# Both MLPs' last down-projection block as seven quarter products, under a written plan for all engines

## The chip, the core and the metric

The kernel runs on one core of a Trainium2 chip. A core has a matrix engine (TensorE, PE in the profile; its weight loads are PEld), a vector engine (VectorE, DVE), a scalar engine (ScalarE, ACT), a general one (GpSimd, POOL) and a sync engine (SyncE, SP) that mostly issues transfers. They run side by side, each through its own queue in order, and wait for one another by semaphores. Data lies in DRAM, in the on-chip SBUF (128 partitions) and in PSUM, eight banks of 128 partitions x 512 fp32 into which PE writes and adds. Sixteen DMA engines move data between DRAM and SBUF; a transfer can also add to what stands at its target (those are issued from POOL).

The metric is the device time of one execution in microseconds (us). It is compared as the median of several runs.

## The reference

Two decoder layers over 512 tokens of width 1024, all in fp32. Layer 0 mixes by latent attention, layer 1 by sliding-window attention; both go on with the same kind of MLP (width 4096) and a LayerNorm after each sublayer:

```python
def _mlp(x, w_up, w_down):
    h = jax.nn.relu(x @ w_up)
    return (h * h) @ w_down

for l in range(DEPTH):
    y = _mla(...) if l < n_a else _swa(...)
    x = _layernorm(alpha * x + y, ln_mix_g[l], ln_mix_b[l])
    x = _layernorm(alpha * x + _mlp(x, mlp_w_up[l], mlp_w_down[l]), ln_mlp_g[l], ln_mlp_b[l])
```

## The kernel before

Each fp32 operand of a product is split into a high part, rounded to the matmul's format (a copy on ACT, L77), and a low part, the difference (a subtraction, L81, on DVE or for some weights on POOL). A product takes three matmuls, high x high, high x low and low x high (`three`), all issued at L105 by `group`.

The MLP walks over its 4096 hidden features in four blocks q of 1024 (`NFF` = 4). In a block, "U" is the up projection and "D" the down projection. Both are made after Strassen's scheme in Winograd's form: tokens and features are cut in halves, the four quarters of each operand are combined by sums, and seven quarter products take the place of eight. They are numbered 1 to 7; `STEPS` is the order in which the steps run, with U' for the next block:

```python
STEPS = "U'1 D5 U'2 D3 U'5 D6 D7 U'3 D4 U'6 U'7 U'4 D'1 D'2"
FIRST_STEPS, LAST_STEPS = "U'1 U'2 U'5 U'3 U'6 U'7 U'4 D'1 D'2", "U'1 D5 U'2 D3 U'5 D6 D7 U'3 U'6 U'7 U'4 D4"
```

`Block.up` (L813) makes a U product of 48 matmuls of 256 columns in two halves and `up_out` (L836) its sums on DVE (L854 to L864), the ReLU and the square on ACT (L867, L868): the four quarters a11, a12, a21, a22 of the hidden activations. `Block.factor` (L871) makes a D product's left factor, a quarter or a sum of quarters (`Factors.sum`, L697: one sum for 5, two for 3, one for 7), split in two. `Block.down_` (L882) makes a D product, 24 matmuls of 512 columns for two token tiles, and adds its result to the tokens `xs` or to `u2` on DVE (L641, L792, L900). The sums of the weights' quarters are made by transfers: a quarter is loaded (SP), split, and the next quarter is added to it in SBUF by a DMA from POOL (L204, `add_more`).

The last block (q = 3) has D products of another kind: the plain product, all four token tiles against all eight weight chunks, made by `TokMajor.finish` (L547). It first makes the left 512 columns of all four tiles, then the right 512 tile by tile, so that the norm of one tile (`layer_norm`, L484: mean and variance by `bn_stats`, L631, and `bn_aggr`, L488; the reciprocal root on POOL, L443; two passes on DVE, L494 and L495) lies beside the product of the next. In layer 1 the last tile's right half is made in two pieces, and `last_norm` (L469) subtracts the mean for the first 512 columns by two matmuls (`ident`, `diag`), scales in three pieces on DVE (L481) and sends each out. In layer 0 the normed tiles are turned by PE (L507, `turn_tokens`) for the next layer, whose first products (w_k, w_v; `begin`, L657) lie between the turns of the last two tiles.

What sets the order: PE and the transfers of SP keep the order in which they are written (`pe`). DVE, ACT and POOL are ordered by a planner that runs when the program is built, by priorities and its own estimates of times; `pin` and `behind` fix single places. Weights come from a list (`stream`) that `weights` prepares at most four chunks ahead; `wh` and `wl` have four buffers each, factors (`fac`) three, PSUM six banks plus two for turns, and the eight large tiles `xt` hold the tokens' parts.

## Time and profile before

| | us |
|---|---|
| median of three runs | 987.31 (987.04 to 987.75) |
| the profiled execution | 986.77 |
| its span, first to last instruction | 985.0 |
| layer 0's MLP in the span, to its last block's U'6 | 206.7 to 436.8 |
| layer 1's MLP in the span, to its last block's U'6 | 681.3 to 911.4 |

The busy table gives each engine's time and share of the span. Matmuls are pipelined, so a PE that is "busy" isn't always at its peak; the chain of work that ended last, followed back from the last instruction, says better what sets the time. A line of that chain in order of time reads: start, length, engine, what it made and its source line, how many instructions. A line of an engine's timeline reads the same way, with operands (out <- in), shapes and, in brackets, the idle time before it and who ended it. A line of the groups has busy time, mean ns of one, idle time before and its releaser. The last figures of a windows row are granted clock, DMA share and GB/s.

### The profile page before, as it was taken

The numbers are of one execution on the slowest core, as the hardware profiler recorded it, in microseconds if no ns is written. First come the engines' busy times: TensorE is split into PE (matmuls) and PEld (weight loads), VectorE is DVE, ScalarE is ACT, GpSimd is POOL, SyncE is SP. The second block draws the span as 40 slices with busy tenths as digits, with TensorE's granted clock in tenths as the row PEclk, the third lists the DMA queues.
The fourth block names the chain that finished last, engine by engine and source line by source line (L and its number), as shares of the span: only waits on it lengthen the run. The fifth ranks groups of instructions, "written<-read, shape, count | busy, mean of one in ns | idle before, by whom it ended". The sixth has DMA issues, their size and how long they took to land.

```text
span 985.0 us, 15665 instructions
## 1 busy us (share of the span) xinstructions
PE 978.4 (99%) x6028; PEld 880.5 (89%) x6028; DVE 773.4 (79%) x1282; ACT 544.7 (55%) x842; POOL 235.7 (24%) x204
## 2 busy tenths in 40 slices
PE   9999999999999999999999999999999999999998
PEld 9888888998999999998898988889998998999986
DVE  6589858999778769887587788898886985888756
ACT  5557644467537637646136787445763763764720
POOL 1231101121212211310002898422221122033000
PEclk9999999999999999999999999999999999999999
DMA  7421236398878968973232212528997796897332
GB/s 264 146 89 44 91 124 199 59 225 218 156 181 235 183 141 237 226 125 120 94 108 86 97 65 98 191 44 181 256 179 134 236 197 117 225 264 140 82 128 86
DMA packets 60678, 149.54 MB, mean 152 GB/s; under 512 B 5259, under 2 KB 10300, under 8 KB 60604
## 3 DMA queue, kind: packets, MB, share of 16 engines
q0 software_dynamic: 24320, 58.73, 33.7%
q1 hardware_dynamic: 36140, 89.56, 26.0%
q8 instruction: 47, 0.77, 0.3%
q10 hardware_dynamic: 144, 0.26, 0.1%
q14 instruction: 27, 0.22, 0.1%
HBM read 146.41 MB, written 4.22 MB: 153 GB/s over the span
## 4 chain that ended last, share of the span: by engine, by line
PE 97%; DVE 2%; POOL 1%; ACT 0%; issue 0%; DVEq 0%; POOLq 0%
PE mm L105 89%; PE tr L105 5%; PE tr L1243 1%; PE tr L742 1%; POOL wl L81 1%; PE tr L1467 0%; PE tr L507 0%; DVE o L1503 0%; DVE mm L1431 0%; DVE pt L81 0%; PE tr L1007 0%; ACT wh L77 0%; DVE mm L1427 0%; PE mm L1148 0%; ACT p L1442 0%
## 5 line engine op out<-in xcount | busy, mean ns | idle before, releaser
L105 PE MATMUL mm<-wh,fac 128*128 128x512 f32 (+1 forms) x944 | 292.7, 386 | 0.0
L77 ACT ACTIVATE wh<-wq 128x1024 fp32r<-128x1024 f32 x164 | 173.7, 1060 | 184.7 <-PE mm L105 137.8
L81 DVE TENSOR_TENSOR wl<-wq,wh 128x1024 fp32r<-128x1024 f32 x164 | 199.2, 1220 | 67.5 <-ACT wh L77 66.6
L105 PE MATMUL mm<-xth,wh 128*128 128x256 f32 (+1 forms) x928 | 243.4, 290 | 0.0
L105 PE MATMUL mm<-xth,wl 128*128 128x256 f32 (+1 forms) x800 | 233.3, 292 | 0.0
L105 PEld LDWEIGHTS mm<-wh,fac 128*128 128x128 f32 x944 | 176.2, 188 | 35.5 <-DVE fac L81 0.6
L105 PE MATMUL mm<-xtl,wh 128*128 128x256 f32 (+1 forms) x672 | 197.1, 293 | 0.0
L105 PE MATMUL mm<-wl,fac 128*128 128x512 f32 (+1 forms) x472 | 182.3, 386 | 0.0
L105 PEld LDWEIGHTS mm<-xth,wh 128*128 128x128 f32 x928 | 168.6, 192 | 3.1
L105 PEld LDWEIGHTS mm<-xth,wl 128*128 128x128 f32 x800 | 153.2, 192 | 2.7
L105 PEld LDWEIGHTS mm<-xtl,wh 128*128 128x128 f32 x672 | 128.7, 191 | 3.0
L77 ACT ACTIVATE wh<-raw 128x1024 fp32r<-128x1024 f32 (+3 forms) x86 | 84.9, 989 | 79.3 <-PE mm L105 57.9
L204 POOL DMA_DIRECT2D wq<-in_up x64 | 77.6, 1238 | 200.3 <-DVE wl L81 193.0
L105 PEld LDWEIGHTS mm<-wl,fac 128*128 128x128 f32 x472 | 88.8, 188 | 16.6
L81 DVE TENSOR_TENSOR wl<-raw,wh 128x1024 fp32r<-128x1024 f32 (+2 forms) x64 | 74.3, 1169 | 30.6 <-ACT wh L77 29.6
L204 POOL DMA_DIRECT2D wq<-in_down x48 | 42.0, 874 | 189.1 <-DVE wl L81 183.2
L81 POOL TENSOR_TENSOR wl<-raw,wh 128x1024 fp32r<-128x1024 f32 (+2 forms) x22 | 47.1, 2143 | 90.8 <-ACT wh L77 65.2
L105 PE MATMUL mm<-wh,oh 128*128 128x512 f32 x128 | 50.7, 396 | 0.0
L105 PE MATMUL mm<-wl,oh 128*128 128x512 f32 x128 | 50.0, 391 | 0.2 <-POOL wl L81 0.2
L105 PE MATMUL mm<-wh,ol 128*128 128x512 f32 x128 | 50.2, 392 | 0.0
L443 POOL TENSOR_TENSOR rs<-mv,half 128x1 f32<-128x1 f32 x16 | 8.8, 552 | 168.1 <-DVE mv L488 163.4
L641 DVE TENSOR_TENSOR x<-mm,x 128x512 f32<-128x512 f32 (+1 forms) x49 | 32.9, 674 | 15.6 <-PE mm L105 15.5
(247 smaller groups left out, 1783.2 us busy)
## 6 DMA issues: line engine op xcount, KB each, us to landing
wq<-in_up POOLq DMA_DIRECT2D x64, 512.0 KB, 7.2
wq<-in_down POOLq DMA_DIRECT2D x48, 512.0 KB, 6.9
wq<-in_up SPq DMA_DIRECT2D x32, 512.0 KB, 6.8
raw<-in_down SPq DMA_DIRECT2D x28, 512.0 KB, 6.1
wq<-in_down SPq DMA_DIRECT2D x24, 512.0 KB, 5.9
raw<-in_up SPq DMA_DIRECT2D x16, 512.0 KB, 4.2
raw<-in_w_o SPq DMA_DIRECT2D x8, 512.0 KB, 3.3
raw<-in_w_sq SPq DMA_DIRECT2D x8, 512.0 KB, 3.2
```

The costliest lines, as they stand in the source:

```text
L77: high = nc.scalar.activation(dst_h, src, AF.Copy)
L81: low = (engine or nc.vector).tensor_sub(dst_l, src, f32(dst_h))
L105: pe(nc.tensor.matmul(dst, st, mv, start=first and i == 0, stop=last and i == len(pairs) - 1, **kw))
L204: state["added", key, a, more, jp] = nc.gpsimd.dma_start(half(a, jp), chunk(*more, jp), accum_op=ALU.add)
L443: state["rs"] = nc.gpsimd.tensor_tensor(r, v, half, ALU.pow)
L641: nc.vector.tensor_add(xs[t][:, c], b, xs[t][:, c])
L742: pe(nc.tensor.transpose(pt[:, a, :], xs[t][:, k * P : (k + 1) * P], ident))
L1243: pe(nc.tensor.transpose(pt[:, kb * P : (kb + 1) * P], p[:, kb * P : (kb + 1) * P], ident))
```

## The change

1. *The last block as quarter products.* A new class `LastBlock` takes the place of `TokMajor.finish` and `Hidden` for both down projections' last block. It makes seven quarter products like the other blocks, but adds them up in PSUM: ACT copies the tokens or `u2` into a bank (`into_bank`, `fill_end`), matmuls add to it, and ACT copies intermediate sums out again (`copy_out`). D4 of block 2 moves ahead of U'6.
2. *A written plan.* The steps from U'6 of the last block to the last norm stand in a list with times, sorted by them; while it is issued, every instruction of DVE, ACT and POOL keeps program order as PE's do.
3. *Low parts on GpSimd.* The low parts of the weights of products 1, 2, 5, 3, 6 and 7 are made by POOL, those of product 4 by DVE; those of w_k move from DVE to POOL. POOL also makes four subtractions of half tiles.
4. *Sums of quarters made in DRAM.* The weights of products 7 and 4 are summed in DRAM ahead of time, by copies on SP and adding DMAs on POOL: layer 0's during its attention, layer 1's during the steps of its own MLP.
5. *The norms.* For the planned tiles DVE centres, ACT scales and POOL adds the offset; the last tile's norm is cut into three column ranges over DVE, ACT and POOL.

```diff
-FIRST_STEPS, LAST_STEPS = "U'1 U'2 U'5 U'3 U'6 U'7 U'4 D'1 D'2", "U'1 D5 U'2 D3 U'5 D6 D7 U'3 U'6 U'7 U'4 D4"
+FIRST_STEPS, LAST_STEPS = "U'1 U'2 U'5 U'3 U'6 U'7 U'4 D'1 D'2", "U'1 D5 U'2 D3 U'5 D6 D7 U'3 D4"
...
+        return lambda *args, **kw: tc.keep_in_program_order(f(*args, **kw))
...
-            for c in range(8):
-                queue("down", io["down"][l, (NFF - 1) * 8 + c])
+            for n in (6, 7, 4):
+                add["U", NFF - 1](n)
+            ends.append(len(stream))
...
         for m in range(2):
-            queue("w_k", io["w_k"][m])
+            queue("w_k", io["w_k"][m], nc.gpsimd)
...
+    lows, early, late = slice(0, 512), slice(512, 768), slice(768, D)
+    for c, to in zip((early, late), b):
+        pe(nc.tensor.matmul(to, diag, gb[0][:, c], start=False, stop=True))
+    nc.vector.scalar_tensor_tensor(x[:, lows], x[:, lows], mv[:, 0:1], gb[0][:, lows], ALU.subtract, ALU.mult)
+    nc.scalar.activation(x[:, early], b[0], AF.Copy, scale=r)
+    nc.gpsimd.tensor_add(x[:, early], x[:, early], gb[1][:, early])
+    for c, src in ((lows, x[:, lows]), (late, b[1])):
+        nc.vector.scalar_tensor_tensor(x[:, c], src, r, gb[1][:, c], ALU.mult, ALU.add)
         nc.sync.dma_start(out[(NT - 1) * P : NT * P, c], x[:, c])
+    nc.scalar.dma_start(out[(NT - 1) * P : NT * P, early], x[:, early])
...
+        def product(self, b, f, t, w, first, cols=slice(0, 512)):
+            tk = slice(t * P, (t + 1) * P)
+            for m in range(4):
+                wh, wl = w[m // 2]
+                c = slice(m % 2 * 512 + cols.start, m % 2 * 512 + cols.stop)
+                group(
+                    b, three(f[:, 0, m, tk], f[:, 1, m, tk], wh[:, c], wl[:, c]), first and m == 0, m == 3,
+                    skip_group_check=True,
+                )
...
+        def fetch(self, n):
+            if n in (7, 4):
+                of = [sum_of(layer, n, jp) for jp in range(2)]
+            else:
+                of = [self.chunk(*{1: (0, 0), 2: (1, 0), 3: (1, 1)}[n], jp) for jp in range(2)]
+            if n in (2, 4):
+                self.raw[n] = [raw_tile().rearrange("p (a b) -> p a b", a=2) for _ in range(2)]
+            else:
+                quad = mp.tile([P, 4, 512], F32, tag="quada" if n == 1 else "quadb", bufs=1, name=nm("wq"))
+                for m in (1, 5, 6) if n == 1 else (n,):
+                    self.raw[m] = [quad[:, 2 * jp : 2 * jp + 2] for jp in range(2)]
+            for jp in range(2):
+                pe(nc.sync.dma_start(self.raw[n][jp], of[jp]))
...
+        def grow(self, n, r, c):
+            for jp in range(2):
+                nc.gpsimd.dma_start(self.raw[n][jp], self.chunk(r, c, jp), accum_op=ALU.add)
+        def high(self, n, jp):
+            if n in (5, 3):
+                pair = tiles_of_weights()
+            else:
+                both = xp.tile([P, 2, 1024], F32R, tag="xt", bufs=8, name=nm("wx"))
+                pair = both[:, 0], both[:, 1]
+            self.w[n][jp] = pair
+            nc.scalar.activation(pair[0], self.raw[n][jp].rearrange("p a b -> p (a b)"), AF.Copy)
+        def low(self, n, jp, engine):
+            wh, wl = self.w[n][jp]
+            engine.tensor_sub(wl, self.raw[n][jp].rearrange("p a b -> p (a b)"), f32(wh))
+        def sum_up(self, n):
+            self.vs = getattr(self, "vs", {})
+            self.vs[n] = self.down.sum(n, *[self.g.get(a) for a in ("a11", "a12", "a21", "a22")])
+        def factor_high(self, n):
+            if n in (1, 2, 4, 6):
+                self.sum_up(n)
+            self.fac[n] = f = mp.tile([P, 2, 4, 256], F32R, tag="fac", bufs=3, name=nm("fac"))
+            nc.scalar.activation(f[:, 0], self.vs[n], AF.Copy)
+        def factor_low(self, n):
+            f = self.fac[n]
+            nc.vector.tensor_sub(f[:, 1], self.vs[n], f32(f[:, 0]))
+        def into_bank(self, key, t, src):
+            nc.scalar.activation(self.bank(("D", key), t), src, AF.Copy)
+        def copy_out(self, key, t, to):
+            nc.scalar.activation(to, self.bank(("D", key), t), AF.Copy)
+        def times(self, n, t, key):
+            self.product(self.bank(("D", key), t), self.fac[n], t, self.w[n], False)
...
+        def moments(self, t):
+            self.mv = getattr(self, "mv", {})
+            self.r = getattr(self, "r", {})
+            self.mv[t] = mv = sp.tile([P, 2], F32, tag="mv", bufs=4, name=nm("mv"))
+            nc.vector.bn_aggr(mv, stats[t])
+            stats[t] = None
+            self.r[t] = rsqrt_of(mv[:, 1:2])
+        def centre(self, t):
+            x = xs[t]
+            nc.vector.scalar_tensor_tensor(x, x, self.mv[t][:, 0:1], self.gb[0], ALU.subtract, ALU.mult)
+        def scale(self, t):
+            nc.scalar.activation(xs[t], xs[t], AF.Copy, scale=self.r[t])
+        def shift(self, t):
+            nc.gpsimd.tensor_add(xs[t], xs[t], self.gb[1])
+            if dst is None:
+                pe(nc.sync.dma_start(out[t * P : (t + 1) * P, :], xs[t]))
...
+        def low_left(self, t, i=0, n=1):
+            c = slice(i * 512 // n, (i + 1) * 512 // n)
+            b = self.ends[t, i]
+            self.product(b, self.fac[4], t, self.w[4], False, c)
+            nc.vector.tensor_add(xs[2 + t][:, c], b, u2[t][:, c])
+            count(2 + t, c)
+        def fill_end(self, t, i=0, n=1):
+            c = slice(i * 512 // n, (i + 1) * 512 // n)
+            self.ends[t, i] = b = bank(512 // n)
+            nc.scalar.activation(b, xs[2 + t][:, c], AF.Copy)
...
+            for i, (n, start) in enumerate(((6, -17.3), (7, -11.5), (4, -5.8))):
+                for half_ in range(2):
+                    at(start + 2.9 * half_, up_half, n, half_)
+                    at(start + 2.9 * half_ + 3.1, self.up_out, n, half_)
+            for time in (-17.2, -14.3, -11.4):
+                at(time, prepare, 1)
+            at(-17.9, self.fetch, 1)
+            at(-12.8, self.fetch, 2)
+            at(-1.5, self.fetch, 3)
+            at(-16.1, self.high, 1, 0)
+            at(-15.1, self.high, 1, 1)
+            at(-15.0, self.low, 1, 0, pool)
+            at(-14.0, self.low, 1, 1, pool)
+            at(-13.0, self.factor_high, 2)
+            at(-12.9, self.grow, 5, 0, 1)
+            at(-6.4, self.high, 2, 0)
+            at(-9.2, self.up_end, 6)
+            at(-7.1, self.factor_high, 1)
+            at(-6.0, self.high, 2, 1)
+            at(-5.4, self.factor_low, 1)
+            for t in range(2):
+                at(-8.0, pool.tensor_sub, xs[t][:, lows], xs[t][:, lows], u2[t])
+                at(-9.0, pool.tensor_sub, xs[2 + t][:, highs], xs[2 + t][:, highs], xs[t][:, highs])
+            at(-5.9, self.low, 2, 0, pool)
+            at(-5.0, self.low, 2, 1, pool)
+            at(-5.9, self.fetch, 4)
+            at(-4.8, self.up_end, 7)
+            at(-4.0, self.factor_low, 2)
+            for t in range(2):
+                at(-6.5, self.into_bank, 1, t, u2[t])
+            at(0.1, vectors)
+            at(0.31, self.high, 5, 0)
+            at(0.32, self.low, 5, 0, pool)
+            at(0.0, self.times, 1, 0, 1)
+            at(0.33, self.high, 5, 1)
+            at(0.34, self.low, 5, 1, pool)
+            at(0.3, self.up_end, 4)
+            at(2.8, self.times, 1, 1, 1)
+            for t in range(2):
+                at(-4.6, self.into_bank, 2, t, xs[t][:, lows])
+            at(3.2, self.sum_up, 5)
+            at(3.25, self.factor_high, 5)
+            at(5.4, self.times, 2, 0, 2)
+            at(5.5, self.factor_low, 5)
+            at(5.5, self.copy_out, 1, 0, u2[0])
+            at(6.2, self.copy_out, 1, 1, u2[1])
+            at(6.3, self.grow, 6, 1, 1)
+            at(6.7, self.sum_up, 3)
+            for jp in range(2):
+                at(4.6 + 1.7 * jp, self.high, 3, jp)
+            at(8.2, self.times, 2, 1, 2)
+            for t in range(2):
+                at(0.5, self.into_bank, 5, t, xs[t][:, highs])
+            at(9.1, self.tops, 0)
+            at(10.1, self.factor_high, 3)
+            at(7.4, self.low, 3, 0, pool)
+            at(7.5, self.low, 3, 1, pool)
+            at(10.4, self.fetch, 7)
+            at(10.9, self.times, 5, 0, 5)
+            for jp in range(2):
+                at(11.2 + jp, self.high, 4, jp)
+            at(12.9, self.factor_low, 3)
+            at(13.3, self.factor_high, 6)
+            at(13.6, self.times, 5, 1, 5)
+            at(13.8, self.tops, 1)
+            at(13.7, lambda: add_plain(2, highs, self.bank(("D", 5), 0)))
+            at(16.7, self.high, 7, 0)
+            at(18.75, self.high, 7, 1)
+            at(19.1, self.low, 7, 0, pool)
+            at(20.5, self.low, 7, 1, pool)
+            at(16.2, self.factor_low, 6)
+            at(16.3, self.times, 3, 0, 5)
+            at(13.4, self.high, 6, 0)
+            at(18.65, self.sum_up, 7)
+            at(13.5, self.high, 6, 1)
+            at(14.7, self.low, 6, 0, pool)
+            at(16.9, self.low, 6, 1, pool)
+            at(16.15, lambda: add_plain(3, highs, self.bank(("D", 5), 1)))
+            at(18.7, self.factor_high, 7)
+            at(19.0, self.times, 3, 1, 5)
+            at(19.7, self.copy_out, 5, 0, xs[0][:, highs])
+            at(19.8, self.factor_low, 7)
+            at(20.4, self.fill_end, 0)
+            at(18.66, self.low, 4, 0, vector)
+            at(18.67, self.low, 4, 1, vector)
+            at(21.8, self.times, 6, 0, 1)
+            at(22.0, self.copy_out, 5, 1, xs[1][:, highs])
+            for i in range(1 + end):
+                at(22.1, self.fill_end, 1, i, 1 + end)
+            at(22.6, self.factor_high, 4)
+            at(26.9, self.factor_low, 4)
+            at(24.5, self.times, 6, 1, 1)
+            at(25.0, self.norm_top, 0)
+            at(25.1, self.moments, 0)
+            at(25.15, self.centre, 0)
+            at(27.2, self.times, 7, 0, 1)
+            at(28.0, self.norm_top, 1)
+            at(29.2, self.moments, 1)
+            at(28.1, self.scale, 0)
+            at(29.1, self.shift, 0)
+            at(29.7, self.centre, 1)
+            at(30.2, self.copy_out, 1, 0, u2[0])
+            at(31.0, self.low_right, 0)
+            at(31.1, self.scale, 1)
+            at(32.1, self.shift, 1)
+            at(32.2, self.low_left, 0)
+            at(34.4, self.moments, 2)
+            at(34.5, self.centre, 2)
+            at(34.6, self.times, 7, 1, 1)
+            at(36.0, self.copy_out, 1, 1, u2[1])
+            at(37.03, self.scale, 2)
+            at(36.1, self.low_right, 1)
+            at(37.1, self.shift, 2)
+            if end:
+                parts = []
+                at(36.2, lambda: parts.extend(last_tokens(self.gb)))
+                for i in range(2):
+                    at(38.0 + i, self.low_left, 1, i, 2)
+                at(40.0, lambda: last_norm(self.gb, *parts))
+            else:
+                def next_weights(n):
+                    state["hold"] = max(state["hold"], state["next"])
+                    prepare(n)
+                at(32.2, next_weights, 2)
+                at(33.0, dst.turn, 0)
+                at(37.0, dst.turn, 1)
+                at(38.0, self.low_left, 1)
+                at(39.0, self.moments, 3)
+                at(39.1, self.centre, 3)
+                at(39.2, self.scale, 3)
+                at(39.3, self.shift, 3)
+                pass
...
+            for _, _, f in sorted(plan, key=lambda x: x[:2]):
+                f()
...
+    extra = sums_at(1, ((2, 2), (8, 14), (20, 20), (26, 32), (37, 43))) if layer else {}
...
+def sum_quarters(i, l, jp):
+    chunk = down(l, NFF - 1)
+    if i == 0:
+        pe(nc.sync.dma_start(sum_of(l, 7, jp), chunk(1, 1, jp)))
+    elif i == 1:
+        nc.gpsimd.dma_start(sum_of(l, 7, jp), chunk(0, 1, jp), accum_op=ALU.add)
+    elif i == 2:
+        pe(nc.sync.dma_start(sum_of(l, 4, jp), sum_of(l, 7, jp)))
+    else:
+        r = (0, 1)[i - 3]
+        nc.gpsimd.dma_start(sum_of(l, 4, jp), chunk(r, 0, jp), accum_op=ALU.add)
...
+    todo = sums_at(0, ((0, 0), (3, 7), (12, 12), (13, 17), (21, 25)))
...
```

266 lines of the change are left out of this document (145 added, 121 removed).

## The prediction

> **What bounds the kernel now.** I read the page's busy table first, then its chain of work that ended last, then that chain in order of time, and last the engines' timelines around the two places where the change works.
>
> ```profile
> span 985.0 us, 15665 instructions
> PE 978.4 (99%) x6028; PEld 880.5 (89%) x6028; DVE 773.4 (79%) x1282; ACT 544.7 (55%) x842; POOL 235.7 (24%) x204
> PE 97%; DVE 2%; POOL 1%; ACT 0%; issue 0%; DVEq 0%; POOLq 0%
> 206.74 5.76 PE tr L105 x48
> 212.50 72.75 PE mm L105 x456
> 493.23 5.46 PE mm L105 x24
> 917.13 61.01 PE mm L105 x336
> 978.17 0.43 DVE x L641
> ```
>
> The chain is TensorE (PE) for 97%: whatever takes work off PE without making PE wait shows in full. In a steady stretch of the MLP (212.50, 456 matmuls) PE never stops. A product of U' is 48 matmuls of 256 columns in 5.76 us, 0.120 each. Twenty-four matmuls of 512 columns of the last block's down projection take 5.46 us (493.23), 0.2275 each. After the last product the end needs 985.0 - 978.14 = 6.9 us of norm and output. The profiled execution took 986.77 us, its span plus 1.8; the median of the runs shown, 987.31, lies 0.5 above it.
>
> **The change, part by part.** *PE.* The last block's down projection was 4 token tiles x 2 halves x 8 x 3 = 192 matmuls of 512 columns. Seven quarter products of 2 x 4 x 3 = 24 make 168. So 24 x 0.2275 = 5.46 us go, twice: **-10.9 us**, if PE is fed as before. D4 of the block before merely moves ahead of U'6, as in the other rows (212.50): nothing.
>
> *What must feed it.* Before, the last block had eight weight chunks of the plainest kind. Now fourteen are split, four factors become seven, and sums (a21-a22 and the like), six low halves on GpSimd (POOL) and the norms join them, in one fixed order on all engines.
>
> ```profile
> 890.48 1.22 DVE L81 TENSOR_TENSOR wl<-wq,wh 128x1024 fp32r<-128x1024 f32 x1
> 891.61 1.22 DVE L81 TENSOR_TENSOR fac<-a,fac 128x1024 fp32r<-128x1024 f32 x1
> 568.31 2.40 POOL L81 TENSOR_TENSOR wl<-raw,wh 128x1024 fp32r<-128x1024 f32 x1
> 570.68 1.28 POOL L81 TENSOR_TENSOR ol<-o,oh 128x512 fp32r<-128x512 f32 x1
> 925.87 1.04 ACT L77 ACTIVATE fac<-a 128x1024 fp32r<-128x1024 f32 x1
> 926.82 1.05 ACT L77 ACTIVATE wh<-raw 128x1024 fp32r<-128x1024 f32 x1
> L845 ACT ACTIVATE uv<-mm 128x512 f32<-128x512 f32 x16 | 9.3, 583 | 5.1 <-PE mm L105 5.1
> L641 DVE TENSOR_TENSOR x<-mm,x 128x512 f32<-128x512 f32 x47 | 32.0, 685 | 14.7 <-PE mm L105 14.6
> L204 POOL DMA_DIRECT2D wq<-in_down x48 | 42.0, 874 | 189.1 <-DVE wl L81 183.2
> wq<-in_down POOLq DMA_DIRECT2D x48, 512.0 KB, 6.9
> ```
>
> Back to back, one starts after the other by 1.13 us (VectorE, DVE), 2.37 (POOL), 0.95 (ScalarE, ACT; 1.0 with a wait), a PSUM addition by 0.6. Six pairs of low halves are 12 x 2.37 = 28.4 us of POOL, whose share in this stage was nearly nil; the question is what they do to DVE.
>
> ```profile
> 628.89 2.38 POOL L81 TENSOR_TENSOR wl<-raw,wh 128x1024 fp32r<-128x1024 f32 x1
> 629.15 3.21 DVE L81 TENSOR_TENSOR w_fac<-wq,w_fac 128x1024 fp32r<-128x1024 f32 x1
> 633.47 1.21 DVE L81 TENSOR_TENSOR w_quada<-wq,w_quada 128x1024 fp32r<-128x1024 f32 x1
> 633.68 3.27 POOL L81 TENSOR_TENSOR wl<-raw,wh 128x1024 fp32r<-128x1024 f32 x1 [2.41 <-ACT wh L77]
> 611.54 1.85 POOL L1471 TENSOR_TENSOR pm<-pt,tri 128x768 fp32r<-128x768 f32 x1
> 612.64 1.83 DVE L81 TENSOR_TENSOR wl<-raw,wh 128x1024 fp32r<-128x1024 f32 x1
> 613.35 2.02 POOL L1451 TENSOR_TENSOR p<-p,ri 128x512 f32<-128x512 f32 x1
> 963.23 1.31 DVE L494 SCALAR_TENSOR_TENSOR x<-x,mv,gb 128x1024 f32<-128x1024 f32 x1
> 963.27 0.56 POOL L443 TENSOR_TENSOR rs<-mv,half 128x1 f32<-128x1 f32 x1 [5.12 <-DVE mv L488]
> 570.30 0.69 DVE L81 TENSOR_TENSOR pt<-tr,pt 128x512 fp32r<-128x512 f32 x1
> ```
>
> The DVE subtraction at 629.15, 1.22 us alone, takes 3.21: it starts its own work when POOL's at 628.89 ends. At 633.68 POOL waits for DVE instead, and 611.54 to 613.35 is a chain of such turns. A DVE operation with one operand in PSUM (570.30, beside POOL's at 568.31) isn't touched. So **a DVE operation with two operands in SBUF and a POOL operation on SBUF go one after the other**, with 0.12 us of overlap at a change. Every sum and low half of a factor is of the first kind, every low half on POOL of the second.
>
> The Trainium skill says the same in SBUF — State Buffer, Who interferes with whom, for a VectorE instruction with two SBUF inputs, and speaks against this change: the second to issue fully blocks until the first finishes. Taken to the letter, without the overlap, it would make the sum below some 4 us longer; and it would hold the tiny POOL power at 963.27 behind the 1.31 us beside it, which the trace doesn't show (0.56).
>
> *The room.* Count from 0, the end of U'4 (U'6 begins at -17.3). DVE's first such operation can start at -16, when the low half of U'7's second weights is due; without a stall quarter product 4 would start at 30.0. By then DVE owes 16 such operations (3 weights of U', 7 factors, 4 sums, 2 weights) and POOL 12 low halves and 4 half-width subtractions: 16 x 1.13 + 12 x 2.37 + 4 x 1.25 = 51.5 us, or 49 with the overlaps, in 46. Were every gap filled, PE would wait 3 to 5.5 us of the 5.46 saved. It can't fill every gap, since each engine keeps its order:
>
> - U'4's second weights wait for their buffer (-11.5), ACT and POOL: DVE is through at -8.2, the three operations on U'6's second half at -6.4. ACT then has, in order, two squared ReLUs of a11 (1.9), factor 1 (1.0), two bank fills (1.2), two weights (2.0), a21 (1.9), two fills (1.2), a22 (1.9): 4.8. The weights of product 5 follow, so POOL starts their low halves at 5.9 and ends at 10.7.
> - Factor 5's low half gets its turn at 10.6, done 11.7; product 2 ended at 10.9: **0.9 late**.
> - POOL issues two adding DMAs (1.8) and takes product 3's low halves to 15.2 and, after a sum of DVE, 18.4. DVE's second sum ends at 16.2, ACT's factor 3 at 17.2, its low half waits for POOL: 19.5. Behind it stands the addition that reads product 5's bank (20.1), which product 3 may only then overwrite; product 5 ended at 17.2: **2.9 late**.
> - From 21.3 POOL has the low halves of 6 (their data landed about 19.4) and 7, DVE five operations: four turns of 2.26 and five of 1.08 with changes end at 35.7 with factor 7; product 6 ended at 31.1: **4.7 late**.
> - One norm's centring and factor 4 end at 39.7; product 7's first half at 38.5: **1.3 late**.
>
> That is 9.8 us per block against 5.46.
>
> *Layer 0's way on.* POOL now ends each norm with a full addition (2.4 for DVE's 1.28) and makes both low halves of w_k; by the same turns the three later turns of tokens wait 0.7, 0.5 and 0.8. Sum: -5.5 + 9.8 + 2.0 = **+6.3**.
>
> *Layer 1's end.*
>
> ```profile
> 979.43 0.55 POOL L443 TENSOR_TENSOR rs<-mv,half 128x1 f32<-128x1 f32 x1 [4.73 <-DVE mv L474]
> 956.88 1.28 POOL L466 TENSOR_TENSOR xg<-x,gb 128x512 f32<-128x512 f32 x1 [45.97 <-DVE x L641]
> 627.63 1.27 POOL L464 TENSOR_SCALAR minus<-ident 128x128 f32<-128x128 f32 x1 [7.38 <-PE mm L105]
> 981.00 0.88 DVE L481 SCALAR_TENSOR_TENSOR x<-mm,rs,gb 128x256 f32<-128x256 f32 x2
> ```
>
> The last reciprocal root was ready 1.8 us after the last product. Now POOL has `minus`, `xg` and token 2's addition (1.3, 1.3, 2.4) queued ahead of it, and the turns end it 5.4 after. The split of the last scaling over three engines gives back one 256-wide operation with its start, 0.6. Sum: -5.5 + 9.8 + 3.5 - 0.6 = **+7.3**.
>
> *Sums in DRAM.* Ten transfers a layer, in stages of which the windows say:
>
> ```profile
> 50.00:100.00 50.00, 50.00 (x273) 42.66 (x272) 45.41 (x140) 32.27 (x78) 12.05 (x8) 1.00 0.20 65
> 830.00:880.00 50.00, 50.00 (x333) 46.19 (x333) 41.39 (x44) 31.36 (x32) 8.42 (x9) 1.00 0.86 223
> q0 software_dynamic: 24320, 58.73, 33.7%
> ```
>
> An adding transfer takes 985 x 33.7% / 112 = 3.0 us of all sixteen engines. Layer 0's lie in the attention (share 0.20). Layer 1's, some 24 us with the copies at half, lie where 0.86 is used of 230 us: 32 us are free. No row shows a DRAM target, so the bounds are nothing and the 24 whole; I take nothing, nearest to the rows, in which PE waits for no transfer.
>
> Also not shown: ACT's copies with a scale (1.06 without; up to 1.25), ACT's writes of a bank that matmuls then add to (0.58), an output DMA on ACT's queue. Each is within 0.2 us of its neighbour, some 1 us of ACT in all, either way.
>
> **Sum:** 986.8 + 6.3 + 7.3 = 1000.4; I forecast **1000.5 us**.
>
> **Rivals.**
> - *The port costs nothing* (the two engines mesh, so that waits fall into gaps). The same walk without turns leaves PE waiting 1.1 us in each block and the end 1.9 late: 986.8 - 10.9 + 1.1 + 1.1 + 1.9 = **980 us**, not slower. For it: DVE idles in this stage, and its PSUM additions are free of POOL. Against: 629.15 and 633.68, and 49 us of turns in 46.
> - *The gaps fill nearly to the bound*: 3 to 5.5 us late per block and 0 to 3 at the end, **982 to 990 us**, about no change. It decides if ACT's backlog at 0 is shorter than counted, so that POOL starts product 5 by 3.
> - *The DRAM sums also collide* in layer 1's MLP: a third of the 24 us exposed, **1008 us**. For it: stretches with a DMA share above 0.9 on the page. Against: no PE wait on DMA today.
> - That the plan isn't kept is no case of its own: every instruction in it is held to the written order.
>
> **How the numbers follow.** Forecast 0.66 (994 to 1006: the walk moved by 1 to 2 us per block when I shifted transfer times, overlaps and starts), port free 0.12, filled gaps 0.06 (two thirds of it no change), collision 0.16. A measurement of this kernel tells 0.2%, 2 us, from no change. Faster 0.12 + 0.02 = 0.14, same 0.04, slower 0.82. The range 985 to 1012 leaves out the free port with the low end of the filled gaps (0.14) and the far end of the collision (0.04).
>
> **What would show it.** Right: PE gaps before the first matmuls of quarter products 3 and 7 in both layers, with DVE subtractions of 3.3 to 3.5 us and POOL's of 2.4 to 3.3 in turns beside them; PE's work less by 48 matmuls of 512 columns; the last `rs` over 4 us after the last product. Wrong: DVE's two-operand work at 1.2 us beside POOL's, or PE gapless in these 55 us; PE waits in layer 1's MLP before its last block would be the DMA's.

## The result, and the profile after

The changed kernel takes 1013.45 us (median of four runs, 1011.36 to 1015.38) where the kernel before takes 987.38 in the same runs: the ratio is 1.0263, with a 95% interval of 1.0236 to 1.0291. The forecast had the sign and the mechanism; 13.6 us of loss were forecast, 26 came. The four executions lie in two groups, 1011.4 to 1011.7 and 1015.2 to 1015.4, and the profile (1011.69 us) is of the lower; a tie between two engines, described below, would fit the difference, but no profile of the upper group shows it. These are lines of its page: span, busy time of the engines, and the chain of work that ended last.

```profile
span 1009.9 us, 15701 instructions
...
PE 977.6 (97%) x5972; PEld 876.4 (87%) x5972; DVE 796.5 (79%) x1266; ACT 583.5 (58%) x897; POOL 357.1 (35%) x266
...
PE 40%; issue 26%; DVE 10%; POOL 10%; DMA 9%; ACT 5%; POOLq 0%; SPq 0%; ACTq 0%; DVEq 0%
```

PE has 56 matmuls less and is hardly shorter busy (977.6 us for 978.4); it held 97% of the chain before and holds 40% now. The time is lost where PE waits. Three rows of PE's timeline (start, duration, line, operation) say by when: U'6 of layer 0's last block, the first product of layer 1's MLP, and U'6 of layer 1's last block.

```profile
442.76 0.28 PE L126 MATMUL tr<-xth,wh 128*128 128x256 f32 x1
...
692.72 0.28 PE L126 MATMUL tr<-xth,wh 128*128 128x256 f32 x1
...
928.22 0.28 PE L126 MATMUL tr<-xth,wh 128*128 128x256 f32 x1
```

In the kernel before they are:

```profile
436.62 0.28 PE L105 MATMUL tr<-xth,wh 128*128 128x256 f32 x1
...
681.17 0.28 PE L105 MATMUL tr<-xth,wh 128*128 128x256 f32 x1
...
911.21 0.28 PE L105 MATMUL tr<-xth,wh 128*128 128x256 f32 x1
```

The first moved by 6.14, of which 5.46 are D4, now ahead of it: 0.7 is lost earlier, most of it in the attention. The second moved by 11.55 and the third by 17.01 - 5.46 = 11.55: layer 0's last block with its way on costs 10.9 of net loss, layer 1's MLP up to its last block nothing, although the DRAM sums run beside it, and the rest, 24.9 - 11.55 = 13.4, is lost in layer 1's last block and the end. (These are net figures: each block has 5.46 us less work.) PE's timeline shows the waits (idle time and releaser in brackets):

```profile
481.39 0.47 PE L126 MATMUL mm<-wh,fac 128*128 128x512 f32 x1 [3.30 <-ACT fac L69]
...
497.54 6.01 PE L126 MATMUL mm<-wx,fac 128*128 128x512 f32 x24 [3.42 <-DVE x L69]
...
509.53 1.83 PE L539 MATMUL tr<-ident,x 128*128 128x128 f32 x8 [2.09 <-DVE xtl L69]
...
969.37 0.76 PE L126 MATMUL mm<-wh,fac 128*128 128x512 f32 x1 [5.85 <-DVE x L69]
969.93 0.63 PE L126 MATMUL mm<-wl,fac 128*128 128x512 f32 x1
970.35 1.05 PE L126 MATMUL mm<-wh,fac 128*128 128x512 f32 x2
971.21 0.63 PE L126 MATMUL mm<-wl,fac 128*128 128x512 f32 x1
...
986.22 12.93 PE L126 MATMUL mm<-wx,fac 128*128 128x512 f32 x60 [3.57 <-DVE x L69]
...
1000.67 1.13 PE L496 MATMUL mm<-xg,ident 128*128 128x256 f32 x4 [1.52 <-POOL xg L69]
```

Product 3 (481.39, 969.37) and product 7 (497.54, 986.22) wait in both layers, as forecast. The bracket of 481.39 is misleading: it names ScalarE's factor 6, which ended at the same time (481.24) as VectorE's addition that reads product 5's bank; in layer 1 the bracket names that addition, and factor 6 ended there (969.90) behind the start of product 3. The rows from 970.35 to 971.21 show something that the forecast lacked: two matmuls of 512 columns take 0.86 us, 0.43 each, where 0.2275 is usual. The windows give the granted clock (the number ahead of the DMA share) there:

```profile
478.00:490.00 12.00, 8.70 (x32) 6.99 (x32) 11.90 (x11) 6.96 (x8) 9.28 (x4) 0.86 0.36 111
...
964.00:976.00 12.00, 6.63 (x20) 5.30 (x21) 11.83 (x13) 6.74 (x7) 5.08 (x2) 0.72 0.35 111
...
988.00:994.00 6.00, 6.00 (x22) 4.81 (x21) 5.86 (x8) 2.04 (x3) 3.88 (x2) 0.75 0.16 66
```

The kernel before, whose span ends at 985.0, has 1.00 in the first two:

```profile
478.00:490.00 12.00, 12.00 (x55) 9.93 (x54) 9.59 (x19) 1.06 (x1) 0.56 (x1) 1.00 0.25 87
964.00:976.00 12.00, 12.00 (x69) 10.56 (x69) 9.49 (x13) 0.00 (x0) 1.09 (x2) 1.00 0.21 87
```

What the products wait for is in the timelines of VectorE and GpSimd. First VectorE, at product 3's operands (layer 0 up to 478, layer 1 after 950):

```profile
472.74 1.23 DVE L69 TENSOR_TENSOR uv<-uv,a 128x1024 f32<-128x1024 f32 x1
474.00 3.31 DVE L69 TENSOR_TENSOR uv<-a,uv 128x1024 f32<-128x1024 f32 x1
...
955.15 3.04 DVE L69 TENSOR_TENSOR fac<-uv,fac 128x1024 fp32r<-128x1024 f32 x1 [2.66 <-ACT fac L69]
958.22 6.49 DVE L69 TENSOR_TENSOR uv<-uv,a 128x1024 f32<-128x1024 f32 x1
964.74 1.22 DVE L69 TENSOR_TENSOR uv<-a,uv 128x1024 f32<-128x1024 f32 x1
...
974.32 3.42 DVE L69 TENSOR_TENSOR uv<-a,a 128x1024 f32<-128x1024 f32 x1
977.66 6.77 DVE L69 TENSOR_TENSOR wx<-raw,wx 128x1024 fp32r<-128x1024 f32 x2
```

And GpSimd's low halves at the same times:

```profile
472.95 6.61 POOL L69 TENSOR_TENSOR wl<-wq,wh 128x1024 fp32r<-128x1024 f32 x2
...
958.21 5.40 POOL L69 TENSOR_TENSOR wl<-wq,wh 128x1024 fp32r<-128x1024 f32 x2
...
970.92 12.42 POOL L69 TENSOR_TENSOR wx<-wq,wx 128x1024 fp32r<-128x1024 f32 x4 [7.31 <-ACT wx L69]
```

The turns are there: subtractions of 1.2 us take 3.0 to 3.4, and four of GpSimd's take 12.4 in place of 9.5. But the two layers differ. In layer 0 VectorE's sum starts 0.21 us ahead of GpSimd's low halves and takes 1.23. In layer 1 it starts 0.01 us behind them and takes 6.49: both of GpSimd's operations, one after the other, and then its own.

### The profile page after: what moved, and what is told of

Read it like the earlier page. It is cut to its first block, busy times and chain, and to the rows that moved or that the text cites. A ratio compares the mean times of both kernels' runs of the same rounds, so it can differ in the third digit from the quotient of the medians.

```text
span 1009.9 us, 15701 instructions
## 1 busy us (share of the span) xinstructions
PE 977.6 (97%) x5972; PEld 876.4 (87%) x5972; DVE 796.5 (79%) x1266; ACT 583.5 (58%) x897; POOL 357.1 (35%) x266
## 4 chain that ended last, share of the span: by engine, by line
PE 40%; issue 26%; DVE 10%; POOL 10%; DMA 9%; ACT 5%; POOLq 0%; SPq 0%; ACTq 0%; DVEq 0%
PE mm L126 35%; POOL wq L226 6%; DMA wq<-in_up 4%; DMA wq<-in_down 3%; DVE uv L69 2%; DVE fac L69 2%; PE tr L126 2%; DVE wx L69 1%; POOL x L69 1%; ACT a L69 1%; DMA sums<-in_down 1%; DVE x L69 1%; PE tr L1542 1%; ACT wh L69 1%; POOL rs L69 1%
## 5 line engine op out<-in xcount | busy, mean ns | idle before, releaser
L97 ACT ACTIVATE wh<-wq 128x1024 fp32r<-128x1024 f32 x158 | 167.3, 1060 | 183.0 <-PE mm L126 135.6
L101 DVE TENSOR_TENSOR wl<-wq,wh 128x1024 fp32r<-128x1024 f32 x158 | 192.3, 1222 | 80.4 <-ACT wh L97 79.9
L126 PE MATMUL mm<-wh,fac 128*128 128x512 f32 x736 | 235.7, 394 | 9.7 <-DVE x L69 5.8
L126 PEld LDWEIGHTS mm<-wh,fac 128*128 128x128 f32 x736 | 140.0, 190 | 40.0 <-ACT wx L69 6.2
L126 PE MATMUL mm<-wl,fac 128*128 128x512 f32 x368 | 145.0, 394 | 0.0
L97 ACT ACTIVATE wh<-raw 128x1024 fp32r<-128x1024 f32 (+3 forms) x68 | 65.8, 970 | 39.1 <-PE mm L126 28.6
L126 PEld LDWEIGHTS mm<-wl,fac 128*128 128x128 f32 x368 | 70.1, 190 | 13.5
L101 POOL TENSOR_TENSOR wl<-raw,wh 128x1024 fp32r<-128x1024 f32 (+2 forms) x22 | 46.7, 2125 | 75.4 <-ACT wh L97 55.3
L126 PE MATMUL mm<-wx,fac 128*128 128x512 f32 (+1 forms) x252 | 59.2, 394 | 7.0 <-DVE x L69 7.0
L126 PEld LDWEIGHTS mm<-wx,fac 128*128 128x128 f32 x252 | 47.2, 196 | 17.5 <-DVE x L69 7.8
L101 DVE TENSOR_TENSOR wl<-raw,wh 128x1024 fp32r<-128x1024 f32 (+3 forms) x46 | 53.5, 1174 | 9.5 <-ACT wh L97 8.1
```

Source lines behind the costliest of these rows:

```text
L97: high = nc.scalar.activation(dst_h, src, AF.Copy)
L101: low = (engine or nc.vector).tensor_sub(dst_l, src, f32(dst_h))
L126: state["mm"] = nc.tensor.matmul(dst, st, mv, start=first and i == 0, stop=last and i == len(pairs) - 1, **kw)
```

## The experiments

All are made from the changed kernel, but the plans further down from one another. Ratios are against the kernel before, run beside each; "profile" is the span of the profiled execution.

| run | median us | ratio (95%) | profile |
|---|---|---|---|
| the change | 1013.45 | 1.0263 (1.0236 to 1.0291) | 1009.9 |
| low halves on VectorE | 1007.98 | 1.0211 (1.0195 to 1.0226) | 1008.0 |
| GpSimd only writes | 990.76 | 1.0035 (1.0022 to 1.0047) | 989.0 |
| PE kept busy | 1013.20 | 1.0262 (1.0244 to 1.0280) | 1013.5 |
| no sums | 1011.63 | 1.0259 (1.0218 to 1.0301) | 1007.9 |
| GpSimd second | 1008.81 | 1.0226 (1.0197 to 1.0256) | 1006.7 |
| last piece by SyncE | 1011.74 | 1.0253 (1.0230 to 1.0276) | 1010.1 |
| other plan | 987.93 | 1.0004 (0.9995 to 1.0014) | 987.0 |
| its order alone | 1012.46 | 1.0250 (1.0234 to 1.0266) | 1011.9 |
| other plan, second | 992.40 | 1.0051 (1.0039 to 1.0064) | 991.7 |
| other plan, third | 992.66 | 1.0060 (1.0047 to 1.0074) | 990.7 |
| other plan, fourth | 985.35 | 0.9979 (0.9970 to 0.9988) | 984.4 |

**GpSimd as busy, but without reading.** This tells the shared port from GpSimd's slowness, its queue and the order.

```diff
-                    engine.tensor_sub(wl, self.raw[n][jp].rearrange("p a b -> p (a b)"), f32(wh))
+                    raw = self.raw[n][jp].rearrange("p a b -> p (a b)")
...
+                    engine.tensor_sub(wl[:, 0:16], raw[:, 0:16], f32(wh)[:, 0:16])
+                    for cols in (1024, 1024, 512):
+                        engine.memset(f32(wl)[:, 16:cols], 0.0)
```

> GpSimd makes of each of those twelve low halves only 16 of 1024 columns, and then writes zeros for as long as the subtraction took (three writes, some 2.3 us in all), so that it waits for the same things and is busy as long, but hardly reads SBUF; the low parts of the weights of six products are left out. Port theory: VectorE's subtractions beside GpSimd's work take 1.2 us, not 3.3; the waits ahead of products 5, 3 and 7 go in both layers (7.5 us and 1.6 of half clock in layer 0, 10.2 and 3.6 in layer 1), those at the turns and at the end stay: 986 to 994 us. Rival (GpSimd is late in its own queue, and its waits or its time hold the products up): its queue runs as before, the waits stay, 1008 us or more.

Measured: 990.76 us. VectorE's timeline and GpSimd's, in the stretch where the change had 3.4 us a turn:

```profile
477.85 1.22 DVE L69 TENSOR_TENSOR fac<-uv,fac 128x1024 fp32r<-128x1024 f32 x1
478.98 1.24 DVE L69 TENSOR_TENSOR uv<-a,a 128x1024 f32<-128x1024 f32 x1
480.15 2.35 DVE L69 TENSOR_TENSOR wx<-raw,wx 128x1024 fp32r<-128x1024 f32 x2
```

And beside it, GpSimd:

```profile
478.35 0.80 POOL L69 TENSOR_TENSOR wx<-wq,wx 128x16 fp32r<-128x16 f32 x1
479.09 2.51 POOL L69 MEMSET wx<- 128x1008 f32 x3
481.56 1.01 POOL L69 TENSOR_TENSOR wx<-wq,wx 128x16 fp32r<-128x16 f32 x1
482.52 2.50 POOL L69 MEMSET wx<- 128x1008 f32 x3
```

GpSimd is busy without a gap, as before; VectorE runs at 1.2 us beside it. The waits of both blocks shrink from 10 and 15 us to under 2 (0.86 us ahead of product 6, and smaller ones). GpSimd's reads carry 22.7 of the 26.1 us (1013.45 to 990.76), and the rival falls; the waits at the turns and in the end stay. The Trainium skill says it so in SBUF — State Buffer, Who interferes with whom: a VectorE instruction with two SBUF inputs contends with a GpSimd instruction that reads SBUF and not with one that only writes. These runs agree (1.21 to 1.24 us beside writes, 3.0 to 3.4 beside reads).

**Low halves on VectorE, in the same order.**

```diff
-                    at(-5.9, self.low, 2, 0, pool)
+                    at(-5.9, self.low, 2, 0, vector)
```

and so for the other eleven.

> The twelve low halves of the weights of products 1, 2, 5, 3, 6 and 7 move from GpSimd to VectorE, at the same places of the written plan, in both layers. Port theory (a VectorE operation with two operands in SBUF and a GpSimd operation on SBUF go one after the other): each low half now costs 1.2 us of VectorE in place of a turn of 2.4, VectorE's subtractions take 1.2 us throughout the stage and none takes 3.3; since VectorE keeps its order, PE then waits ahead of products 1, 5, 3 and 4 (2.4, 1.4, 2.2 and 2.3 us by the walk) and no longer ahead of 7, each wait under the 3 us after which the clock was seen to halve: 997 to 1004 us. Rival (PE waits for the written order and for ScalarE's queue, and GpSimd's work is beside the point): the waits ahead of products 3 and 7 stay at 3.5 to 6 us, and VectorE, with 13.6 us more work a block, makes it 1013 us or more.

Measured: 1007.98, above the range and below the rival's time. PE's waits moved; in layer 0 they are 1.3 and 3.6 us at the two halves of U'4, 1.7 ahead of product 3, 1.4 ahead of product 7. VectorE's queue holds a low half of product 2, which waits for ScalarE, ahead of the additions that free U'4's bank (`[3.41 <-DVE a L69]` in PE's timeline). That is the order's price, not the port's. So the order alone was tried too, with another plan.

**Another plan, and its order alone.** The other plan gives VectorE eleven of fourteen low halves, and some sixty places of the list are changed; it was found with the walk of the prediction. It also makes the scaling and the offset of three tokens' norms in layer 0, and of one in layer 1, in one operation of VectorE, and the run with its order alone does so too.

```diff
+                    times = {
+                        'high 1 0': -16.65, 'low 1 0': -16.61, 'high 1 1': -12.15, 'low 1 1': -10.31, 'grow 5 0 1': -9.69,
...
+                    on_pool = ((1, 1), (6, 0), (7, 0))
```

> The same quarter products under another written plan: eleven of the fourteen low halves on VectorE (GpSimd keeps one of product 1, 6 and 7 each), some sixty of VectorE's, ScalarE's and GpSimd's operations at other places of the list, the scaling and the offset of tokens 0, 2 and 3 in layer 0 and of token 2 in layer 1 in one operation of VectorE, and the constant minus made early. PE's order and all transfers but their issue times are as in the change. Port theory, by the walk that met the waits of the runs with the low halves on VectorE and with GpSimd only writing: hardly a wait of PE in either block (0.2 to 1 us each; in the change 10 and 15), the later turns 1 to 2 us, the end 1 us earlier: 982 to 988 us. Rival (quarter products with their splits can't be fed within the block by these engines, in whatever order): 3 us or more of waits in each block and 993 us or more.

> The other plan of the run before (987.9 us), but all twelve low halves of the weights of products 1, 2, 5, 3, 6 and 7 on GpSimd, as in the change: its order alone. With the run that had the low halves on VectorE under the change's own order (1008.0 us), this makes the four combinations whole. Port theory (the turns fill the stage, whatever the order): by the walk PE waits 11 to 12 us in each block ahead of products 1, 3, 6 and 7, 1006 to 1018 us. Rival (the change's order was what was wrong, and the engine of the low halves matters little): under 995 us.

Measured: 987.93 for the plan (its upper bound), 1012.46 for its order with all twelve low halves on GpSimd, where PE waits 4.75 us in product 1 and less ahead of 3, 6 and 7. With the two runs above: own order 1013 (GpSimd) and 1008 (VectorE), other order 1012 and 988. With these two orders neither the engine nor the order does it alone; both together take 25 us. (The other order was sought for low halves on VectorE; none was sought anew for GpSimd.) In the plan's block PE waits only at U'4, 1.7 us in each layer at the longest: VectorE's low half of product 2 there took 4.28 us, behind two of GpSimd's half-width subtractions, and held up the additions behind it.

**Who is first.** The near tie in layer 1 was broken by a write of GpSimd ahead of its first low half.

```diff
                     wh, wl = self.w[n][jp]
+                    if (n, jp) == (3, 0):
+                        engine.memset(f32(wl)[:, 0:320], 0.0)
```

> GpSimd writes zeros into 320 columns (0.35 us) ahead of the first low half of product 3, and then the whole low half over them; nothing else is changed. In the change the two engines reach that place together: VectorE's sum for factor 3 started 0.21 us ahead of GpSimd's low half in layer 0 (sum 1.23 us), and 0.01 us behind it in layer 1 (sum 6.49 us, over two of GpSimd's operations). Theory (whoever of the two is first by a hair decides, and VectorE, when it starts within some 0.05 us behind GpSimd, loses two turns in place of one): with GpSimd 0.35 us later VectorE is first in both layers, the sum takes 1.2 us in both, PE waits some 3.5 us ahead of product 3 in both, and all executions lie together near the lower ones of the change: 1008 to 1012 us, spread under 1.5 us. Rival (GpSimd's two low halves of product 3 are always ahead of the sum in layer 1, for instance since its transfers come later): layer 1 keeps the sum of 6.5 us, and the time and its spread stay at 1011 to 1015 us.

Measured: 1008.81; three of four executions within 1008.4 to 1009.2, the fourth at 1014.1, which stays unexplained. The sum in layer 1, and GpSimd beside it:

```profile
958.26 1.23 DVE L69 TENSOR_TENSOR uv<-uv,a 128x1024 f32<-128x1024 f32 x1
959.52 3.30 DVE L69 TENSOR_TENSOR uv<-a,uv 128x1024 f32<-128x1024 f32 x1
...
958.23 1.01 POOL L69 MEMSET wl<- 128x320 f32 x1
959.32 5.73 POOL L69 TENSOR_TENSOR wl<-wq,wh 128x1024 fp32r<-128x1024 f32 x2
```

The write took 1.01 us, not 0.35, and GpSimd's low halves start 1.1 us later than in the change (959.32 for 958.21), clearly behind VectorE's sum. Product 3 now waits 3.30 us in layer 1 as in layer 0 (`[3.30 <-ACT fac L69]`; the engine named is again factor 6's), product 7 waits 5.00 in place of 3.57, and the profile is 3.2 us shorter, with more work in it. The theory holds in this trace; the medians, 1008.81 and 1013.45, have intervals that overlap.

**Is the half clock paid?**

```diff
                 def times(self, n, t, key):
+                    if t == 0 and n in (3, 7):
+                        b = tbank().rearrange("p (a b) -> p a b", a=4)
+                        group(b, [(zeros, zeros[:, None, :].broadcast_to([P, 4, P]))] * 13)
```

> Thirteen matmuls of zeros (512 columns, 3.0 us at full clock) into a spare bank stand ahead of product 3 and of product 7 in both layers; nothing else is changed, and their time fits into the waits of 3.3 to 6 us. Clock theory (the granted clock halves after a PE stall of some 3 us, and the matmuls behind it take 0.43 us each in place of 0.23): with the stalls filled the clock stays 1.00 after them, which gives back 1.6 us in layer 0 (product 3) and 1.4 to 3.6 in layer 1 (products 7 and 3; product 3's stall of 5.9 us is filled by half only): 1006 to 1010 us. Rival (the slow matmuls have another cause, such as their weights or banks): they stay slow, and the time is that of the change, 1011 to 1015 us.

Measured: 1013.20, as the change. The clock did stay up in layer 1, as the windows show:

```profile
964.00:976.00 12.00, 9.19 (x41) 7.29 (x40) 11.83 (x12) 6.46 (x7) 4.69 (x3) 1.00 0.59 151
982.00:988.00 6.00, 5.40 (x24) 4.12 (x22) 6.00 (x3) 4.46 (x8) 4.90 (x2) 1.00 0.00 0
```

And yet nothing came back. From the start of product 3 to that of product 7 it is 972.90 to 989.77, 16.87 us; in the change's layer 1, with 11 matmuls at half clock between, 969.37 to 986.22, 16.85. From there to the end it is 23.7 us in both. VectorE and GpSimd set the start of product 7, so the slow matmuls only fill a wait that is there anyway. Both theories missed: the clock stays up with PE kept busy, and the half clock costs nothing here. (Layer 0's tie fell the other way in this run: its sum took 6.47 us, 0.05 behind GpSimd. The span is 3.6 us longer, 2.5 of it by the start of layer 1's MLP; the rest is 1.05 in that MLP, where a low half came late behind a load, `[0.70 <-DVE wl L101]` at 810.15. None of the other profiles shows a wait there.)

**The sums, and the last transfer.**

```diff
-                    if n in (7, 4):
-                        of = [sum_of(layer, n, jp) for jp in range(2)]
-                    else:
-                        of = [self.chunk(*{1: (0, 0), 2: (1, 0), 3: (1, 1)}[n], jp) for jp in range(2)]
+                    of = [self.chunk(*{1: (0, 0), 2: (1, 0)}.get(n, (1, 1)), jp) for jp in range(2)]
...
-            for i, pair in enumerate(when):
+            for i, pair in enumerate(when[:0]):
```

> The sums of quarters in DRAM are left out (ten transfers of each layer), and products 7 and 4 load a plain quarter of the weights instead; so the products 7 and 4 have other weights than they should. Theory (the sums lie beside transfers and PE work that hide them): within 1 us of the change, at most the 0.5 us that layer 0's attention was longer comes back. Rival of the prediction (the sums collide with layer 1's loads, or GpSimd's issuing of them holds up others): 2 us or more come back.

Measured: 1011.63, with an interval that covers the change's. Inconclusive at 1 to 2 us by the median; by the trace of the change itself layer 1's MLP isn't longer by anything up to its last block, and that excludes the rival's place. The profile without the sums agrees: this stretch takes 235.51 us (691.42 to 926.93), with them 235.50. It is 2.0 us shorter as a whole, 0.4 ahead of layer 0's last block, 0.9 between that block and layer 1's MLP and 0.7 behind it; whether the sums cost that is open.

```diff
-            nc.scalar.dma_start(out[(NT - 1) * P : NT * P, early], x[:, early])
+            nc.sync.dma_start(out[(NT - 1) * P : NT * P, early], x[:, early])
```

> The last tile's middle columns leave by SyncE's queue again, not by ScalarE's; nothing else is changed. In the change the last computing instruction ends 4.6 us before the end of the execution, before it was 3.1. Theory (an output transfer from ScalarE's queue ends later than one from SyncE's): 3.1 to 3.4 us from the last computing instruction to the end, 1.2 to 1.5 us off the time, which the spread of the change may hide in the median but not in the profile. Rival (the 1.5 us come from the later computing of that piece or from three transfers at once): 4.6 us stay.

Measured: 1011.74. The last operation of the computing and the transfer behind it, in the timeline:

```profile
1004.71 0.78 POOL L69 TENSOR_TENSOR x<-x,gb 128x256 f32<-128x256 f32 x1 [0.59 <-ACT x L69]
...
1005.83 0.40 SPq L510 DMA_DIRECT2D out<-x  x1
```

The last computing ends at 1005.49, the span at 1010.1: 4.6 us stay, and the theory falls. What the 1.5 us are by which this is longer than in the kernel before (3.1) is open.

**The other plan, mended.** Three more versions went after its waits. All have a few spare matmuls of zeros ahead of the last norm, which keep the clock up. The second has a list found anew for both layers, of which this is its load and GpSimd's share:

```diff
-                    on_pool = ((1, 1), (6, 0), (7, 0))
+                    on_pool = ((1, 1), (4, 1), (6, 0))
...
-                    at(-5.9, self.fetch, 4)
+                    at(-1.4, self.fetch, 4)
```

> The other plan again, mended where its run still waited: VectorE's low halves of product 2 stand behind the outputs of U'7 (2.2 us of PE waiting in each layer there), the load of product 4's weights behind that of product 3's, token 2's last operation in layer 1 behind the last tile's first piece (the last mean came 1.1 us late behind it), the low halves of w_k behind the turn of token 0, and eleven matmuls of zeros keep PE busy in the end (the last four matmuls ran at half clock there, 1 us). GpSimd keeps one low half each of products 1, 4 and 6. Expected from these waits: 2.2 + 2.2 + 1.1 + 0.8 us and what the turns give (0.5 to 1), 979 to 984 us, faster than both kernels. Rival (each removed wait shows the next one behind it, as filling PE did): 985 to 988 us, no change against before.

The third has that load too, but takes its list from the first plan, with product 2's low halves behind factor 1's; in layer 0 it changes some fifteen places of the norms, factor 4 and w_k's weights besides:

```diff
-                        'factor_low 1': -1.01, 'low 2 0': -5.93, 'low 2 1': -4.65,
+                        'factor_low 1': -2.6, 'low 2 0': -2.5, 'low 2 1': -2.4,
```

> The first other plan (987.9 us) with only its own waits mended: VectorE's low halves of product 2 stand behind the outputs of U'7 and U'4's first half and behind factor 1 (so that none of them meets GpSimd's four half-width subtractions by a hair), product 4's weights are loaded behind product 3's, the turns of layer 0 stand ahead of the split of w_k (VectorE makes the offsets of tokens 1 to 3 there), token 2's last operation in layer 1 stands behind the last tile's first piece, and eleven matmuls of zeros keep PE busy in the end. Theory (PE is the bound again, so that every wait removed counts in full): 2.2 us in each layer at U'4, 0.5 to 1.5 at the turns, 1 to 2 in the end, 980 to 984 us. Rival (the second other plan, 992.4 us, showed it already: what is moved meets the next wait): 986 us or more, and the profile shows a new wait of 2 us or more in a block.

Measured: 992.40 and 992.66, slower than the plan they mended, though the block behind U'4 hardly waits. Both are above the ranges expected; of the third the rival came out, with its new wait. Rows of the third plan's timeline (SyncE's queue, ScalarE, PE):

```profile
435.99 0.89 SPq L970 DMA_DIRECT2D wq<-in_down  x2
...
447.75 1.06 ACT L69 ACTIVATE wh<-wq 128x1024 fp32r<-128x1024 f32 x1 [3.12 <-DMA wq<-in_up]
...
456.22 0.76 PE L126 MATMUL mm<-xth,wh 128*128 128x256 f32 x2 [2.13 <-DVE a L69]
```

Both plans load product 4's weights behind product 3's. Product 3's had stood behind product 4's, which waits for a buffer, and were issued at 461.38 in the first plan. Now nothing holds them, and they run at 435.99 beside the adding transfer that completes U'4's first weights (issued at 439.65). ScalarE waits 3.12 us for these (1.15 in the first plan), U'4 2.1 to 3.3, and here PE hardly waits again behind it, so the half clock (15 and 27 matmuls of 0.21 us in layer 0) is paid too. The fourth plan holds that load back by a real dependency:

```diff
+                        if n == 3:
+                            for jp in range(2):
+                                nc.vector.memset(quad[:, 2 * jp, 0:1], 0.0)
...
-                    at(-1.5, self.fetch, 3)
+                    at(-3.5, self.fetch, 3)
```

> The run before (992.7 us) with one thing changed: the load of product 3's weights (two transfers of 512 KB) waits for a VectorE write of one column behind the outputs of U'7. In the two runs before, where the load of product 4's weights no longer stood ahead of it, it was issued some 8 us earlier, beside the adding transfer that completes U'4's first weights; these came 1.1 to 2.6 us later than in the plan of 987.9 us, PE waited 2.3 to 3.5 us ahead of U'4, and its clock halved behind that (25 matmuls of 0.21 us in place of 0.12 in layer 0). Theory (the earlier transfer is what collided): U'4's weights are there as in the first other plan or earlier, the waits ahead of U'4 are under 0.5 us in both layers and the clock stays 1.00, 982 to 985 us, faster than both kernels. Rival (VectorE's order is what makes U'4 late): the waits of 2 us and more stay, 990 us or more.

Measured: 985.35, 0.2% faster than the kernel before, and the fastest version here; it lies just above its range. The load is issued at 456.52 (it had been 25 us early, not the 8 of the expectation), the wait ahead of U'4 is 0.8 us in layer 0 and gone in layer 1, and the mean granted clock is 0.999. Of the 10.9 us that the quarter products save, 2.1 arrive by the medians and 0.6 in the profile. There 1.5 us are lost ahead of layer 0's last block, 4.1 in it and on the way to layer 1's MLP, 1.0 in layer 1's last block, and 3.8 in the end, which takes 10.7 us from the last product (973.7 to 984.4) where the kernel before needs 6.9. No single wait of PE in the blocks and at the turns is over 1.1 us.

## Why the prediction was wrong in its size

*The saving and the mechanism* were right. PE's work fell, the waits stand ahead of products 3 and 7 in both layers, VectorE's subtractions take 3.0 to 3.4 us in turns with GpSimd's, and without GpSimd's reads of the weights the loss shrinks from 26 to 3.4 us. "The port costs nothing" is excluded, and so is a collision of the sums in layer 1's MLP in the change's profile.

*The walk through the block* had 0.9, 2.9, 4.7 and 1.3 us of waiting ahead of products 5, 3, 7 and 4, 9.8 in sum. Measured from start to start of PE's matmuls:

| wait ahead of | U'4 | 5 | 3 | 7 | 4 | half clock | sum |
|---|---|---|---|---|---|---|---|
| forecast | 0 | 0.9 | 2.9 | 4.7 | 1.3 | 0 | 9.8 |
| layer 0 | 0.9 | 0.4 | 3.5 | 3.6 | 0 | 1.6 | 9.9 |
| layer 1 | 0.9 | 0.4 | 6.0 | 3.7 | 0 | 3.6 | 14.7 |

Layer 0's block came out as forecast in sum, and that is partly luck: 1.6 us of half clock and 0.9 ahead of U'4, which the forecast lacked, and 0.6 more ahead of product 3 stand where 1.3 ahead of product 4, 1.1 ahead of 7 and 0.5 ahead of 5 didn't come. Two steps of the sum failed: product 3 in layer 1, and layer 0's way on. **Product 3 in layer 1**: the walk gave the port to whoever came first and let the two alternate ("2.9 late"). VectorE's sum came 0.01 us behind GpSimd and lost two turns; the wait was 6.0, 3.1 more than forecast, and breaking the tie took 3.2 us off the profile. That an addition behind factor 7's low half, not the low half itself, releases product 7, and that product 4 doesn't wait behind it, moved waits between neighbours. The half clock was missing from the forecast altogether, though the kernel before has matmuls of 512 columns at 0.42 us in its first 5 us (with the granted clock at 1.00 there); in the block it turned out to cost nothing, since VectorE and GpSimd set the next start, and without it the wait ahead of product 7 would be longer.

**Layer 0's way on**: 2.0 forecast, 5.3 measured (2.25 ahead of the second tile's turn, 1.2 ahead of a later one, 0.2, and some 1.6 of half clock in the turns). The walk had the turns wait for the normed tokens, which GpSimd's additions finished at 508.7 and 523.7. PE went on only 0.8 and 1.8 us later, at 509.53 and 525.51, because it also waits for the low parts of the tile turned before (`<-DVE xtl`), which the prediction doesn't mention. At 509.53 these came late since ScalarE made a scaling and two high halves of w_k (505.06 to 508.11) ahead of their high part; at 525.51 they stood in VectorE's queue behind a low half of a weight that took 2.60 us in a turn with GpSimd. The half clock isn't what costs here: with GpSimd second the turns have none, and they start at 509.52 and 525.50 all the same. What holds the turns is read from the trace; no run tests it alone. Some 1.1 more lie outside, 0.7 ahead of layer 0's MLP and 0.4 in layer 1's first turn; their cause is open.

*Layer 1's end*: 2.9 forecast, 3.9 measured. The root comes 4.8 us behind the last product (5.4 forecast), as these rows of GpSimd show: each waits for VectorE or for what the list put ahead of it.

```profile
997.30 1.53 POOL L69 TENSOR_TENSOR rs<-mv,half 128x1 f32<-128x1 f32 x1
998.82 0.55 POOL L69 TENSOR_SCALAR minus<-ident 128x128 f32<-128x128 f32 x1
999.36 1.26 POOL L69 TENSOR_TENSOR xg<-x,gb 128x512 f32<-128x512 f32 x1
1000.59 2.33 POOL L69 TENSOR_TENSOR x<-x,gb 128x1024 f32<-128x1024 f32 x1
1002.89 1.01 POOL L69 TENSOR_TENSOR rs<-mv,half 128x1 f32<-128x1 f32 x1
```

What was wrong is the last scaling: it was to give back 0.6, and from the root to the end it is 6.0 us in place of 5.0.

Sum of the misses: 3.3 (turns) + 4.9 (layer 1's block) + 1.0 (end) + 1.1 (outside the blocks) + 0.7 (small ones) = 11.0 of the 11.3 between 13.6 and the profile's 24.9.

## What to carry to other kernels

A share of 35% on an engine says nothing about what its operations take away from another: count the operations of both that need one resource, and see whether the stage has room for the sum. With a fixed order on all engines, neither another engine nor another order helped much alone here; both together took 25 us. An operation or a load that is moved ahead meets what was hidden there: a load 25 us earlier made weights late that nobody had touched.

## What the runs showed of the hardware

- **A near tie costs VectorE two turns.** Where a VectorE operation on two SBUF tiles and a GpSimd operation with a second one behind it start within 0.07 us of each other, VectorE waited for both of GpSimd's in nine places (6.46 to 6.49 us in five, 4.2 to 4.3 in four with half-width operations) and ran at once in three (1.22 to 1.23). It was first by 0.01 us or less in those three, but also in three of the nine. At 0.2 to 0.5 us behind it waited for one (3.0 to 3.3).
- **The clock halves after short waits.** In the change's trace waits of 3.3, 2.1, 5.9 and 3.6 us were followed by stretches at half clock (granted clock 0.50), some at once, some about 1 us later; one of 3.4 (497.54) was not. Three of the stretches last some 3.5 us (482.3 to 485.8, 509.6 to 513.1, 987.5 to 990.9), the one at the longest wait 6.7 (967.1 to 973.8). The Trainium skill, TensorE: Matmul & The Clock Gate, What's actually happening, gives at least one idle window of about 3.4 us for it, in windows that run freely; the 2.1 us are less than that.
- A reading GpSimd operation of 16 columns takes 0.22 us alone and up to 1.2 beside VectorE's on two SBUF tiles (0.80 and 1.01 in the rows above): it waits for its turn like a large one.
